# Gathered copies and ones-sums in the score ladder of a hybrid decoder layer

## The chip, the cores and the metric

The kernel runs on one core of a Trainium2 chip. The metric is device time in microseconds (us), the median of several runs; lower is better. One execution was profiled, and all durations below come from its trace.

## The reference

One decoder layer on x of 2048 tokens by 1024 channels, in float32: RMS norm, a wide projection, two groups of heads side by side, an output projection, then a gated MLP with a causal convolution and a final norm. The part that the change touches is the HGRN2 group, four heads with keys and values of 128:

```python
f = lb + (1.0 - lb) * jax.nn.sigmoid(hf)
k_hg = 1.0 - f
# S_t = diag(f_t) S_{t-1} + k_t v_t^T,  o_t = S_t^T q_t
o_hg = hgrn2_chunkwise(q_hg, k_hg, v_hg, log_f)
o_hg = rmsnorm(o_hg, hg_norm_w[l])
o_hg = o_hg * jax.nn.silu(hg)
```

Within a block of tokens the output of token t is a sum over earlier tokens s of a score times v_s, and the score is the sum over the 128 key channels of q_t * k_s times the product of all f between s and t. The second group is sliding-window attention with sinks (eight heads of 64, window 128).

## The kernel before

The 2048 tokens are worked off in two halves of 1024 (`hf`). Each half has a mix stage (attention and HGRN2 heads), then the output projection, gate and up, and down. All large matmuls split a float32 operand into a high and a low part of the type fp32r (a float32 form that the TensorE multiplies in one pass) and add three products; names ending in hi/lo, whi/wlo, XH/XL are such parts. A matmul of plain float32 shows two records in the trace.

In the mix stage `hgrn` and `attend` are generators, one of each per head `h` (0 to 3), advanced in turn. A planner inside the framework then sets the order of the instructions on each engine from its own cost estimates; the engines wait for each other through semaphores, and each engine works strictly in its order. So the order has to be read from the built program.

One head of `hgrn`: projections `f` and `hq` give f and q with the 128 key channels on partitions and 1024 tokens along the row; K = 1 - f and Q = q * f. The scores ST, eight blocks of 128 by 128 tokens, are filled in pieces:

- The diagonal (s = t): float32 matmuls of K with q per block into `pdiag` (L544), of which only the diagonal is kept (L545, a product with the identity).
- A ladder of levels m = 1, 2, 4 ... 64 (`LEVELS`). At level m tokens stand in pairs of neighbouring groups of m: the later group takes its scores from Q, the earlier from K. Matmuls write them to `plev`; then Q of the later groups and K of the earlier ones are multiplied by the running products of f (L609, L610), f is folded to half its length (L616), and the next level follows. So level 2m needs the products of level m.
- For m below 32, heads 0 to 2 work in pairs (`pairs`, `place_pairs`): ScalarE copies the needed half of K of two blocks into `KK` (L566), and four 128x128 matmuls serve eight blocks (L569). Half of the result lies m partitions too low; ScalarE copies it to `moved` (L576), a DMA on ScalarE's queue shifts it into `odd` (L579, and L581 for level 1), and VectorE places it with a mask (L588), the other half directly (L585). The last head doesn't pair: eight matmuls with 64 columns per level (L602), placed by L625.
- m = 32 and 64: small matmuls per block (L607), copied by ScalarE (L630).

Afterwards Kn is K transposed (`pkn`, L640), pu = Kn v (L647), the states SS follow, and per block two products go into `po` (L665, L666), each followed by its square with a sum over the row (L667). Their norm, a transposition (`pot`) and the gate give the head's output.

Beside it on TensorE stand the projections (`f`, `hq`, `q`, `g`, L212), `project_v` for two heads at once (`pvv`, L698 to L700, with 24 matmuls of 256 columns per block of tokens, evicted by ScalarE, L702), the attention (`psc` scores, `ppt` transpositions, `poT` outputs) and, at the stage's end, the output projection (`pop`). All score groups use the two PSUM banks of the pool "hg".

Of the kernel before, what the change touches and what calls it, by code (L numbers as in the profile page):

```python
# [43 lines left out]
KB = 2  # L44
# [6 lines left out]
def hymba_layer(ctx: ExitStack, tc: tile.TileContext, a: dict, out: bass.AP):  # L51
# [18 lines left out]
    def ps(kind, name):  # L70
        return spaces[kind].tile([P, 512], F32, tag=kind, name=name)
# [12 lines left out]
    nc.gpsimd.memset(eps, EPS)  # L84
    ident = cp.tile([P, P], F32, name="ident")
# [434 lines left out]
    def hgrn(hf, h, X, invb, vs, WG, mix, p, fu=None):  # L520
# [12 lines left out]
        K = p.tile([P, HALF], F32, tag="K", name="K", bufs=1)  # L533
        nc.vector.tensor_scalar(K, f, -1.0, 1.0, op0=ALU.mult, op1=ALU.add)
        Q = p.tile([P, HALF], F32, tag="Q", name="Q", bufs=1)
# [4 lines left out]
        for b in range(NB):  # L540
            pd = ps("hg", "pdiag")
            for i in range(4):
                c = slice((b * 4 + i) * P, (b * 4 + i + 1) * P)
                nc.tensor.matmul(pd[:, i * P:(i + 1) * P], K[:, c], q[:, c], start=True, stop=True)  # L544
            nc.vector.tensor_tensor(ST[:, 4 * b:4 * b + 4], pd.rearrange("p (i t) -> p i t", i=4),  # L545
                                    ident.unsqueeze(1).to_broadcast([P, 4, P]), op=ALU.mult)

# [12 lines left out]
        F, left = f, None  # L560

        def pairs():


            KK = p.tile([P, HALF // 2], F32, tag="KK", name="KK", bufs=KB)
            nc.scalar.copy(KK.rearrange("p (r b c m) -> p r c b m", r=TT // 2, c=2, m=m),  # L566
                           K.rearrange("p (r c b w m) -> p r c b w m", c=2, b=nbc, w=2, m=m)[:, :, :, :, 0])
            for r in range(TT // 2):
                marks[m] = nc.tensor.matmul(pl[:, r * P:(r + 1) * P], KK[:, r * P:(r + 1) * P],  # L569
                                            Qv[:, 2 * r * nbc:2 * (r + 1) * nbc, 1], start=True, stop=True)  # L570

        def place_pairs():

            plv = pl.rearrange("p (r c t) -> p r c t", r=TT // 2, c=2)
            moved, odd = [p.tile([P, TT // 2, 64], F32, tag="lv", name=n, bufs=LV) for n in ("moved", "odd")]
            nc.scalar.copy(moved, plv[:, :, 1])  # L576

            rows_ = P - max(m, 2)
            nc.scalar.dma_start(odd[0:rows_], moved[m:m + rows_])  # L579
            if m == 1:  # L580
                nc.scalar.dma_start(odd[rows_:rows_ + 1], moved[P - 1:P])  # L581
            STv = ST.rearrange("p (r c) (b w m) -> p r c b w m", c=2, w=2, m=m)
            mk = C.lmask[m].bitcast(U32).rearrange("p (b m) -> p b m", m=m)
            mk = mk.unsqueeze(1).to_broadcast([P, TT // 2, nbc, m])
            nc.vector.copy_predicated(STv[:, :, 0, :, 1], mk, plv[:, :, 0].rearrange("p r (b m) -> p r b m", m=m))  # L585
            r = slice(0, P - m)
            ov = odd[r].rearrange("p r (b m) -> p r b m", m=m)
            return lambda: nc.vector.copy_predicated(STv[r, :, 1, :, 1], mk[r], ov)  # L588

        for m in LEVELS:  # L590
            nb = HALF // (2 * m)
            nbc = 64 // m
            Qv = Q.rearrange("p (b w m) -> p b w m", w=2, m=m)
            Kv = K.rearrange("p (b w m) -> p b w m", w=2, m=m)
            Fv = F.rearrange("p (b w) -> p b w", w=2)
            pl = ps("hg", "plev")
            paired = m < 32 and h < HG - 1
            if paired:
                pairs()
            elif m < 32:  # L600
                for c in range(TT):
                    marks[m] = nc.tensor.matmul(pl[:, c * 64:(c + 1) * 64], K[:, c * P:(c + 1) * P],  # L602
                                                Qv[:, c * nbc:(c + 1) * nbc, 1], start=True, stop=True)
            else:
                for c in range(TT):
                    for s0 in range(0, P, 2 * m):
                        nc.tensor.matmul(pl[s0:s0 + m, c * m:(c + 1) * m], K[:, c * P + s0:c * P + s0 + m],  # L607
                                         Q[:, c * P + s0 + m:c * P + s0 + 2 * m], start=True, stop=True)
            nc.vector.tensor_tensor(Qv[:, :, 1], Qv[:, :, 1], Fv[:, :, 0:1].to_broadcast([P, nb, m]), op=ALU.mult)  # L609
            done = nc.vector.tensor_tensor(Kv[:, :, 0], Kv[:, :, 0], Fv[:, :, 1:2].to_broadcast([P, nb, m]), op=ALU.mult)  # L610
# [10 lines left out]
            if paired:  # L621
                left = place_pairs()
            elif m < 32:
                mk = C.lmask[m].bitcast(U32).rearrange("p (b m) -> p b m", m=m)
                nc.vector.copy_predicated(ST.rearrange("p c (b w m) -> p c b w m", w=2, m=m)[:, :, :, 1],  # L625
                                          mk.unsqueeze(1).to_broadcast([P, TT, nbc, m]),
                                          pl.rearrange("p (c b m) -> p c b m", c=TT, m=m))
            else:
                for s0 in range(0, P, 2 * m):
                    nc.scalar.copy(ST[s0:s0 + m, :, s0 + m:s0 + 2 * m],  # L630
                                   pl[s0:s0 + m, 0:TT * m].rearrange("p (c m) -> p c m", c=TT))
        yield
# [28 lines left out]
        for c in range(TT):  # L661
# [5 lines left out]
            nc.scalar.activation(on[:, c], o, AF.Square, accum_out=ss[:, c:c + 1])  # L667
# [626 lines left out]
```

## Time and profile before

| | |
|---|---|
| median of 3 runs | 2198.23 us (2197.66 to 2200.65) |
| profiled execution, first to last instruction | 2198.0 us |
| mean granted TensorE clock | 0.997 |
| TensorE (PE) busy | 2180.4 us, 99% |
| VectorE (DVE) busy | 1639.5 us, 75% |
| ScalarE (ACT) busy | 1049.9 us, 48% |
| mix stage of half 0 around the change | 68.2 to 402.0 us |
| mix stage of half 1 around the change | 1158.2 to 1495.0 us |

How rows are read: "L609 DVE TENSOR_TENSOR Q<-Q,f ..." is the code line, the engine, the operation, and what is written from what, with buffer numbers left out; then come the shapes (partitions x elements), the count, busy time and the mean of one in ns, and the idle time before with what ended it. In the timeline the first number is the start, the second the length, both in us. Waits are "engine line <- releaser: total, times, longest". POOL (GpSimd) is busy 6.3 us in all and plays no part. The profiled span lies 0.2 us under the median.

### The profile page before, as it was taken

What the parts mean: (1) busy time and instruction counts of PE and PEld (TensorE: products, weight loads), DVE (VectorE), ACT (ScalarE), POOL (GpSimd) and SP (SyncE); (2) the same over time, 40 slices, a digit from 0 to 9 for tenths busy, and PEclk for the clock granted to TensorE, in tenths of its full rate; (3) what the DMA queues carried; (4) which work ended last, traced back from release to release, by engine and by line L of the source; (5) the groups of instructions that cost most, each with busy time, mean ns of one, the idle gap of its engine ahead of it and who ended that gap; (6) DMA issues with size and microseconds to landing.
All of it is one profiled execution on the core that took longest, in us unless ns stands there. A gap on an engine that the chain in (4) does not pass through costs nothing.

```text
span 2198.0 us, 29524 instructions
## 1 busy us (share of the span) xinstructions
PE 2180.4 (99%) x11424; PEld 1834.0 (83%) x11424; DVE 1639.5 (75%) x2451; ACT 1049.9 (48%) x1848; POOL 6.3 (0%) x28
## 2 busy tenths in 40 slices
PE   9999999999999999999999999999999999999998
PEld 7988988888888888888889889888888888888888
DVE  6567568688887888885855666677888878887766
ACT  6445544454444445335735455544644444443353
POOL 1000000000000000000000000000000000000000
PEclk9999999999999999999999999999999999999999
DMA  4101112323333234964631111114132323259643
GB/s 155 51 32 48 39 41 68 119 74 102 104 109 108 89 127 143 372 241 156 209 125 41 44 36 51 58 39 134 58 125 92 125 91 109 98 183 393 233 144 130
DMA packets 94358, 257.91 MB, mean 117 GB/s; under 512 B 11594, under 2 KB 17546, under 8 KB 94218
## 3 DMA queue, kind: packets, MB, share of 16 engines
q1 hardware_dynamic: 88992, 251.30, 33.9%
q10 hardware_dynamic: 5226, 4.73, 0.7%
q8 instruction: 89, 1.46, 0.3%
q14 instruction: 51, 0.42, 0.1%
HBM read 195.10 MB, written 57.15 MB: 115 GB/s over the span
## 4 chain that ended last, share of the span: by engine, by line
PE 95%; DVE 3%; ACT 1%; DMA 1%; issue 0%; SPq 0%; DVEq 0%; ACTq 0%
PE X L877 7%; PE X L878 7%; PE X L879 7%; PE pop L212 7%; PE hq L212 4%; PE q L212 4%; PE f L212 4%; PE g L212 4%; PE Y L879 4%; PE Y L878 4%; PE Y L877 4%; PE pdx L1088 3%; PE pdx L1089 3%; PE pdx L1090 3%; PE pdy L1089 3%; PE pdy L1088 3%
## 5 line engine op out<-in xcount | busy, mean ns | idle before, releaser
L706 ACT CAST whi<-raw 128x1024 fp32r<-128x1024 f32 x88 | 92.6, 1053 | 109.2 <-PE X L878 68.2
L877 PE MATMUL X<-T,whi 128*128 128x512 f32 x352 | 136.9, 389 | 0.0
L878 PE MATMUL X<-T,whi 128*128 128x512 f32 x352 | 136.9, 389 | 0.0
L879 PE MATMUL X<-T,wlo 128*128 128x512 f32 x352 | 136.9, 389 | 0.0
L972 DVE SCALAR_TENSOR_TENSOR y<-ga,cw,y 128x1024 f32<-128x1024 f32 x88 | 112.5, 1281 | 26.0 <-ACT y L970 26.0
L884 ACT COPY u<-X 128x512 f32<-128x512 f32 x88 | 51.4, 585 | 133.3 <-PE X L879 133.1
L707 DVE TENSOR_TENSOR wlo<-raw,whi 128x1024 fp32r<-128x1024 f32 x88 | 107.3, 1220 | 0.0
L190 ACT CAST whi<-raw 128x1024 fp32r<-128x1024 f32 x57 | 59.5, 1048 | 93.1 <-PE q L212 31.9
L707 DVE TENSOR_TENSOR xld<-raw,xhd 128x1024 fp32r<-128x1024 f32 x72 | 80.8, 1133 | 19.1 <-ACT xhd L706 18.9
L706 ACT CAST xhd<-raw 128x1024 fp32r<-128x1024 f32 x72 | 69.7, 978 | 43.6 <-DMA raw<-act0T 14.8
L212 PE MATMUL pop<-XL,whi 128*128 128x512 f32 x256 | 86.1, 396 | 2.1 <-DVE XL L224 2.1
L212 PE MATMUL pop<-XH,wlo 128*128 128x512 f32 x256 | 85.2, 393 | 0.8 <-DVE wlo L191 0.8
L212 PE MATMUL pop<-XH,whi 128*128 128x512 f32 x256 | 84.5, 397 | 0.2
L878 PEld LDWEIGHTS X<-T,whi 128*128 128x128 f32 x352 | 66.1, 188 | 13.7
L877 PEld LDWEIGHTS X<-T,whi 128*128 128x128 f32 x352 | 66.1, 188 | 13.7
L879 PEld LDWEIGHTS X<-T,wlo 128*128 128x128 f32 x352 | 66.1, 188 | 13.7
L1088 PE MATMUL pdx<-xhd,hid 128*128 128x512 f32 x192 | 74.4, 391 | 1.0 <-ACT hid L706 1.0
L1089 PE MATMUL pdx<-xld,hid 128*128 128x512 f32 x192 | 74.7, 389 | 0.0
L1090 PE MATMUL pdx<-xhd,lod 128*128 128x512 f32 x192 | 73.7, 389 | 0.0
L698 PE MATMUL pvv<-whi,XH 128*128 128x256 f32 x256 | 73.5, 288 | 0.0
L191 DVE TENSOR_TENSOR wlo<-raw,whi 128x1024 fp32r<-128x1024 f32 x57 | 69.5, 1222 | 4.2 <-ACT whi L190 4.1
L699 PE MATMUL pvv<-whi,XL 128*128 128x256 f32 x256 | 72.6, 284 | 0.0
(379 smaller groups left out, 6563.3 us busy)
## 6 DMA issues: line engine op xcount, KB each, us to landing
wr<-in_w_down SPq DMA_DIRECT2D x90, 512.0 KB, 4.8
raw<-in_w_gate SPq DMA_DIRECT2D x44, 512.0 KB, 3.6
raw<-in_w_up SPq DMA_DIRECT2D x44, 512.0 KB, 3.6
raw<-act0T SPq DMA_DIRECT2D x20, 512.0 KB, 6.1
raw<-act1T SPq DMA_DIRECT2D x20, 512.0 KB, 10.1
act0B<-y SPq DMA_DIRECT2D x33, 256.0 KB, 2.6
act1B<-y SPq DMA_DIRECT2D x33, 256.0 KB, 2.4
raw<-in_w_out SPq DMA_DIRECT2D x16, 512.0 KB, 4.7
```

The costliest lines, as they stand in the source:

```text
L212: marks["unit"] = nc.tensor.matmul(o[b], w, x[:, bs], start=f, stop=l)
L698: nc.tensor.matmul(o[:, 0:256], xh[:, t], hi[:, c], start=kt == 0, stop=False)
L699: nc.tensor.matmul(o[:, 0:256], xl[:, t], hi[:, c], start=False, stop=False)
L706: return (nc.scalar.copy(h, src), (eng or nc.vector).tensor_tensor(l, src, h.bitcast(F32), op=ALU.subtract))
L707: (eng or nc.vector).tensor_tensor(l, src, h.bitcast(F32), op=ALU.subtract))
L877: nc.tensor.matmul(o, wh[:, ws], xh, start=i == 0 and not more, stop=False, skip_group_check=more)
L878: nc.tensor.matmul(o, wh[:, ws], xl, start=False, stop=False, skip_group_check=more)
L879: r = nc.tensor.matmul(o, wl[:, ws], xh, start=False, stop=i == 3, skip_group_check=more)
L972: nc.vector.scalar_tensor_tensor(y, g[:, w:w + HALF], C.cw[:, ft, w:w + 1], y, op0=ALU.mult, op1=ALU.add)
L1088: nc.tensor.matmul(o, wh[:, i, c], ah[:, i, cols], start=f, stop=False, skip_group_check=more)
L1089: nc.tensor.matmul(o, wh[:, i, c], al[:, i, cols], start=False, stop=False, skip_group_check=more)
L1090: nc.tensor.matmul(o, wl[:, i, c], ah[:, i, cols], start=False, stop=l, skip_group_check=more)
```

## The change

It does five things in `hgrn`:

1. Q and K become two halves of one tile QK, and per level one VectorE instruction (`own`) multiplies both in place of two.
2. At every level from 2 on ScalarE copies the needed parts of both Q and K into a gathered tile G (two buffers), and the matmuls read G alone, in all four heads with pairing: four 128x128 matmuls at levels 2 to 16 and also at 64, sixteen small ones at 32. A pair now joins block c with block c + 4 instead of two neighbours.
3. The diagonal and level 1, in which each token has one partner, become element products on VectorE (`dd`), split into fp32r high and low parts (cast on ScalarE, difference on VectorE), and summed over the channels by two fp32r matmuls of 512 columns with a matrix of ones: two such groups for the diagonal, one for level 1. Level 1 needs no shift and no DMA.
4. The eight squares of `po` stand in a loop of their own behind all products.
5. The tiles' room comes from a smaller dynamic DMA scratch (256 bytes).

```diff
-KB = 2
+GB = 2
...
+    ones_r = cp.tile([P, P], F32R, name="ones_r")
+    nc.vector.memset(ones_r.bitcast(F32), 1.0)
...
-        K = p.tile([P, HALF], F32, tag="K", name="K", bufs=1)
+        QK = p.tile([P, 2, HALF], F32, tag="QK", name="QK", bufs=1)
+        Q, K = QK[:, 0], QK[:, 1]
...
-        for b in range(NB):
-            pd = ps("hg", "pdiag")
-            for i in range(4):
-                c = slice((b * 4 + i) * P, (b * 4 + i + 1) * P)
-                nc.tensor.matmul(pd[:, i * P:(i + 1) * P], K[:, c], q[:, c], start=True, stop=True)
+        def summed_products(x, y):
+            d = p.tile([P, 512], F32, tag="dd", name="dd", bufs=2)
+            hi, lo = [p.tile([P, 512], F32R, tag="dg", name=n, bufs=4) for n in ("dh", "dl")]
+            nc.vector.tensor_tensor(d, x, y, op=ALU.mult)
+            nc.scalar.copy(hi, d)
+            nc.vector.tensor_tensor(lo, d, hi.bitcast(F32), op=ALU.subtract)
+            o = ps("hg", "pdiag")
+            nc.tensor.matmul(o, ones_r, hi, start=True, stop=False)
+            marks[1] = nc.tensor.matmul(o, ones_r, lo, start=False, stop=True)
+            return o
+        for b, bs in halves():
+            pd = summed_products(q[:, bs], K[:, bs])
...
+            if m > 1:
+                G = p.tile([P, 2, HALF // 2], F32, tag="G", name="G", bufs=GB)
+                nc.scalar.copy(G.rearrange("p t (b c m) -> p t b c m", c=2, m=m), far)
...
+                    for r in range(R):
+                        x = slice(r * P, (r + 1) * P)
+                        marks[m] = nc.tensor.matmul(pl[:, x], G[:, 1, x], G[:, 0, x], start=True, stop=True)
             else:
+                pl = summed_products(Q.rearrange("p (b w) -> p b w", w=2)[:, :, 1], K.rearrange("p (b w) -> p b w", w=2)[:, :, 0])
-            nc.vector.tensor_tensor(Qv[:, :, 1], Qv[:, :, 1], Fv[:, :, 0:1].to_broadcast([P, nb, m]), op=ALU.mult)
-            done = nc.vector.tensor_tensor(Kv[:, :, 0], Kv[:, :, 0], Fv[:, :, 1:2].to_broadcast([P, nb, m]), op=ALU.mult)
+            done = nc.vector.tensor_tensor(own, own, Fv.rearrange("p b w -> p w b").unsqueeze(3).to_broadcast([P, 2, nb, m]),
+                                           op=ALU.mult)
...
-            nc.scalar.activation(on[:, c], o, AF.Square, accum_out=ss[:, c:c + 1])
+        for c in range(TT):
+            nc.scalar.activation(on[:, c], po[c // 4][:, c % 4 * P:(c % 4 + 1) * P], AF.Square,
+                                 accum_out=ss[:, c:c + 1])
...
-    nc = bacc.Bacc("TRN2", target_bir_lowering=False, num_devices=1)
+    nc = bacc.Bacc("TRN2", target_bir_lowering=False, num_devices=1, dynamic_dma_scratch_size=256)
```

`far` is the view of QK that holds the later groups of Q and the earlier groups of K, with block c beside block c + 4; `place` moves and places a level as `place_pairs` did.

The planner orders the mix stages anew; outside them TensorE's order is the same row for row. Three places of the built order follow; tile names carry their buffer numbers where rows would read alike.

TensorE, first head of the first half, from the end of the projection q to the first pvv. Before:

```order
L212 MATMUL q1_544<-XL_276,whi_539 128x512
L212 MATMUL q0_543<-XH_275,wlo_540 128x512
L212 MATMUL q1_544<-XH_275,wlo_540 128x512
L544 MATMUL pdiag_615<-hg0_533,K_610 128x128 x4
L544 MATMUL pdiag_621<-hg0_533,K_610 128x128 x4
L698 MATMUL pvv_746<-whi_600,XH_146 128x256
```

Now, at the same place:

```order
L214 MATMUL q1_546<-XL_278,whi_541 128x512
L214 MATMUL q0_545<-XH_277,wlo_542 128x512
L214 MATMUL q1_546<-XH_277,wlo_542 128x512
L550 MATMUL pdiag_622<-dh_617,ones_r_87 128x512
L551 MATMUL pdiag_622<-dl_618,ones_r_87 128x512
L550 MATMUL pdiag_632<-dh_627,ones_r_87 128x512
L551 MATMUL pdiag_632<-dl_628,ones_r_87 128x512
L706 MATMUL pvv_745<-whi_602,XH_148 128x256
L707 MATMUL pvv_745<-whi_602,XL_149 128x256
```

Eight float32 matmuls have become four of fp32r in the same place; they now wait for VectorE's products and ScalarE's casts.

TensorE, last head of the first half, in the ladder (levels 4 and 8 before; levels 32 and 64 now), among attention and output projection. Before:

```order
L212 MATMUL pop1_3627<-XH_3134,wlo_3546 128x512
L602 MATMUL plev_3164<-Q_3037,K_3035 128x64 x8
L495 MATMUL ppt_3395<-ident_87,sc_3239 128x128 x4
L495 MATMUL ppt_3404<-ident_87,sc_3239 128x128 x4
L602 MATMUL plev_3177<-Q_3037,K_3035 128x64 x8
L506 MATMUL poT_3411<-po_3393,V_443 64x128
```

And now:

```order
L214 MATMUL pop1_3633<-XL_3123,whi_3551 128x512
L214 MATMUL pop0_3632<-XH_3122,wlo_3552 128x512
L604 MATMUL plev_3211<-G_3209 32x32 x16
L461 MATMUL psc_3314<-KS_444,qh_3308 128x256
L461 MATMUL psc_3314<-KS_444,ql_3309 128x256
L609 MATMUL plev_3235<-G_3233 128x128 x4
```

Before, a level of this head is eight matmuls and the ladder reaches to the transpositions of the attention (ppt); now a level is four, and the ladder ends while the attention still makes its scores (psc).

VectorE, third head, in the ladder from the product of level 8 on (the product is L609 and L610 before, L612 now; the last number of its shape is m). Before:

```order
L609 TENSOR_TENSOR Q<-Q,f 128x64x8
L477 TENSOR_SCALAR m<-m 128x8
L585 COPY_PREDICATED ST<-lmask_324,plev 128x4x8x8
L616 TENSOR_TENSOR f<-f 128x64
L610 TENSOR_TENSOR K<-K,f 128x32x16
L588 COPY_PREDICATED ST<-lmask_324,odd 120x4x8x8
L552 TENSOR_TENSOR hg_2081<-g_2670,invb 128x512
L552 TENSOR_TENSOR hg_2081<-g_2671,invb 128x512
L484 TENSOR_TENSOR den<-den,es 128x8
L485 RECIPROCAL den<-den 128x8
L468 COPY_PREDICATED sc<-own,psc 128x256
```

And now:

```order
L612 TENSOR_TENSOR QK<-QK,f 128x2x64x8
L586 COPY_PREDICATED ST<-lmask_318,odd 126x128x2
L619 TENSOR_TENSOR f<-f 128x64
L583 COPY_PREDICATED ST<-lmask_322,plev 128x64x4
L612 TENSOR_TENSOR QK<-QK,f 128x2x32x16
L586 COPY_PREDICATED ST<-lmask_322,odd 124x64x4
L583 COPY_PREDICATED ST<-lmask_326,plev 128x32x8
L619 TENSOR_TENSOR f<-f 128x32
L612 TENSOR_TENSOR QK<-QK,f 128x2x16x32
L586 COPY_PREDICATED ST<-lmask_326,odd 120x32x8
L583 COPY_PREDICATED ST<-lmask_330,plev 128x16x16
```

The levels follow each other closely now, and placements of shifted rows (L586, the tile odd) stand between two products where gate and attention work stood before.

73 lines of the change are left out of this document (32 added, 41 removed).

## The prediction

> **What bounds the kernel now.** I read the page's totals first, then its chain, then the two stages that the change touches, then what TensorE waits for in them.
>
> ```profile
> PE 2180.4 (99%) x11424; PEld 1834.0 (83%) x11424; DVE 1639.5 (75%) x2451; ACT 1049.9 (48%) x1848; POOL 6.3 (0%) x28
> ...
> PE 95%; DVE 3%; ACT 1%; DMA 1%; issue 0%; SPq 0%; DVEq 0%; ACTq 0%
> ```
>
> TensorE is busy 2180.4 of 2198.0 us and carries 95% of the chain that ends last. The changed code runs only in the two mix stages. The built orders of before and after agree row for row on TensorE outside them, so I cut the span there (columns: length, then PE, PEld, DVE, ACT, POOL busy, granted clock, DMA share, GB/s):
>
> ```profile
> 68.20:402.00 333.80, 331.64 (x2289) 289.05 (x2289) 224.35 (x440) 166.81 (x429) 0.00 (x0) 0.99 0.15 45
> ...
> 1158.20:1495.00 336.80, 334.72 (x2316) 291.59 (x2315) 225.68 (x439) 167.30 (x430) 0.00 (x0) 0.99 0.16 47
> ```
>
> TensorE is full there too (331.64 of 333.80, 334.72 of 336.80), VectorE at 67% and ScalarE at 50%. All that it waited for in these stages over 0.3 us, first stage, then second (total, times, longest):
>
> ```profile
> PE pop L212 <- DVE XL L224: 0.7, 1, 0.7
> PE plev L602 <- DVE K L610: 0.7, 1, 0.7
> ...
> PE pop L212 <- DVE XL L224: 1.4, 1, 1.4
> ```
>
> So the stage's length is the sum of its matmuls. A matmul taken away there is time taken away, as long as nobody feeds TensorE later than now.
>
> **What TensorE is spared.** I price a group by start to start: from its first matmul to the next other one, plus what that next one is late against its usual pitch. One plain fp32r 128x512 costs 10.88/48 = 0.227 us:
>
> ```profile
> 57.54 10.88 PE q L212 x48
> ```
>
> Score diagonal before (a float32 matmul leaves two records, so 8 make x16):
>
> ```profile
> 68.26 1.95 PE L544 MATMUL pdiag<-hg,K 128*128 128x128 f32 x16
> ...
> 69.96 0.36 PE L698 MATMUL pvv<-whi,XH 128*128 128x256 f32 x1
> ...
> 70.16 0.28 PE L699 MATMUL pvv<-whi,XL 128*128 128x256 f32 x1
> ```
>
> 69.96 - 68.26 = 1.70, and the next start follows after 0.20 where 0.12 is usual: 1.78 us. A pair-wise level, and the usual pitch of pvv (0.12):
>
> ```profile
> 73.52 0.28 PE L698 MATMUL pvv<-whi,XH 128*128 128x256 f32 x1
> 73.64 1.07 PE L569 MATMUL plev<-Q,KK 128*128 128x128 f32 x8
> 74.46 0.36 PE L699 MATMUL pvv<-whi,XL 128*128 128x256 f32 x1
> 74.66 0.28 PE L700 MATMUL pvv<-wlo,XH 128*128 128x256 f32 x1
> ```
>
> 0.82 + 0.08 = 0.90 us. A level of the last head, which isn't paired before:
>
> ```profile
> 346.72 1.90 PE L602 MATMUL plev<-Q,K 128*128 128x64 f32 x16
> 348.43 0.73 PE L212 MATMUL pop<-XL,whi 128*128 128x512 f32 x2
> 349.00 0.61 PE L212 MATMUL pop<-XH,wlo 128*128 128x512 f32 x2
> ```
>
> 1.71, and the two pop take 0.57 where 0.45 is usual: I take 1.79 (0.08 as above). Level 64:
>
> ```profile
> 99.01 1.15 PE L607 MATMUL plev<-Q,K 128*64 128x64 f32 x16
> 100.08 0.38 PE L459 MATMUL psc<-KS,ql 128*128 128x256 f32 x1
> 100.31 0.28 PE L459 MATMUL psc<-KS,qh 128*128 128x256 f32 x1
> ```
>
> 1.07 + 0.11 = 1.18 us. Now per head and half, 8 in all, 6 of them paired before:
> - diagonal: 1.78 becomes four fp32r 128x512, 0.91: 8 x 0.87 = 7.0
> - level 1: 0.90 (6 times) or 1.79 (twice) becomes two such matmuls, 0.45: 6 x 0.45 + 2 x 1.34 = 5.4
> - levels 2 to 16 of the last head: four groups of 1.79 become four of 0.90: 2 x 4 x 0.89 = 7.1
> - level 64: 1.18 becomes a group like a pair level, 0.90: 8 x 0.28 = 2.2
> - level 32 keeps 16 small matmuls, the other heads' levels 2 to 16 keep four 128x128: 0.
>
> Sum 21.7 us. The third term has a rule against it. By the Trainium skill, page "TensorE: Matmul & The Clock Gate", section "Back-to-back issue gap", a matmul's spacing grows with its streamed columns, so 64 columns would cost half of 128, halving the count would spare nothing, and the sum would be 14.6 (2183.4 us). The rows above deny it: 1.71/16 = 0.107 us per 64-column record, 0.82/8 = 0.103 per 128-column one. The same page's section on LDWEIGHTS (128 weight columns take 107 ns) fits them.
>
> **What the other engines get.** Prices:
>
> ```profile
> L536 DVE TENSOR_TENSOR Q<-hg,f 128x1024 f32<-128x1024 f32 x8 | 9.8, 1220 | 8.3 <-PE po L666 8.3
> L545 DVE TENSOR_TENSOR ST<-pdiag,ident 128x512 f32<-128x512 f32 x16 | 10.8, 688 | 11.5 <-PE pdiag L544 11.5
> L609 DVE TENSOR_TENSOR Q<-Q,f 128x512 f32<-128x512 f32 x56 | 38.6, 690 | 30.9 <-PE plev L569 18.6 <-PE plev L607 11.8 <-PE plev L602 0.4
> ...
> L585 DVE COPY_PREDICATED ST<-lmask,plev 128x256 f32<-128x256 uint32 x30 | 16.6, 554 | 3.4 <-ACT moved L576 3.3
> ```
> ```profile
> L706 ACT CAST whi<-raw 128x1024 fp32r<-128x1024 f32 x88 | 92.6, 1053 | 109.2 <-PE X L878 68.2 <-issue 19.1 <-PE Z L878 13.8
> ...
> L566 ACT COPY KK<-K 128x512 f32<-128x512 f32 x30 | 19.1, 636 | 29.6 <-DVE K L610 21.2 <-DVE K L534 8.2
> L667 ACT ACTIVATE on<-po 128x128 f32<-128x128 f32 x64 | 17.6, 275 | 58.3 <-PE po L666 56.9
> ...
> L576 ACT COPY moved<-plev 128x256 f32<-128x256 f32 x30 | 11.1, 371 | 23.8 <-PE plev L569 23.4
> ```
>
> VectorE, per head: fourteen products of 0.69 become seven of 1.22 (-1.1); three element products and three subtractions come (+4.1); placing stays within 1 us. That is +3 to +4, some 25 us over both stages: 475 of 649 us, 73%. ScalarE, per paired head: five copies of 0.64 become six gathers of 1.05 and three casts of 0.64 come, less one moved copy: +4.7; in the last head, which had none of it, +9.7; together 48 us, 382 of 649, 59%. Not in the trace is a gather or a level's product of 1024: between 1.05 (a plain cast of that size) and twice KK, 1.27; between 1.22 (Q from q and f, plain) and twice 0.69, 1.38. I take the lower ends, since KK and Q with their gaps already cost what plain ones of 512 do. Neither engine becomes the bound by its sum, so I cost both at nothing on the path; the cover is TensorE's own queue of projections, and if it runs out the price is the wait itself. ScalarE's queue issues six DMAs that shift rows per paired head now (two at level 1) and four then; the last head goes from none to four. SyncE's queue keeps its loads in nearly the same order and no load is added. ones_r is one memset ahead of the first load's landing: nothing. The smaller scratch moves no instruction.
>
> The ladder is where cover could end. A gather needs the previous level's product; with two G buffers the gather of level 8 also waits for level 2's matmuls. From there to level 64's matmuls a head needs four gathers, three products and seven handoffs, 8.6 us (4.2 + 3.7 + 0.7; 10.0 by the upper prices). A handoff I take as 0.1; K, which is done at 81.47 in the VectorE rows below, had its copy start at 81.50, and level 32 costs TensorE 0.63 + 0.10 = 0.73:
>
> ```profile
> 81.50 0.62 ACT L566 COPY KK<-K 128x512 f32<-128x512 f32 x1 [0.20 <-DVE K L610]
> ```
> ```profile
> 94.38 0.70 PE L607 MATMUL plev<-Q,K 128*32 128x32 f32 x32
> 95.01 0.38 PE L698 MATMUL pvv<-whi,XH 128*128 128x256 f32 x1
> 95.23 0.28 PE L699 MATMUL pvv<-whi,XL 128*128 128x256 f32 x1
> ```
>
>  TensorE's order puts between these two points, in the third head (the tightest), 70 pvv x 0.12 + three levels x 0.90 + level 32 0.7 = 11.8 us; by the same count some 14 in the first head and more in the other two. Spare in the third: 3.2 us, of which three moved copies (1.1), four evictions of v and the DMA issues on ScalarE eat most, partly beside VectorE's products. So it holds, by 1 or 2 us.
>
> What a shifted level costs the queue behind it: VectorE's placement of the shifted rows waits for a DMA, and the next product stands behind it.
>
> ```profile
> 78.89 0.73 DVE L609 TENSOR_TENSOR Q<-Q,f 128x512 f32<-128x512 f32 x1
> ...
> 80.78 0.69 DVE L610 TENSOR_TENSOR K<-K,f 128x512 f32<-128x512 f32 x1
> 81.79 0.74 DVE L588 COPY_PREDICATED ST<-lmask,odd 126x256 f32<-126x256 uint32 x1 [0.33 <-DMA odd<-moved]
> ```
>
> The level's matmuls were done at 78.89, the rows had landed at 81.79: 2.9 us with the copy (0.37), so 2.5 for issue and landing. It stands within the 11.8.
>
> Squares behind the products: eight squares, 8 x 0.28 plus their accumulator reads, now start together after the last product instead of beside it; rsqrt and pot come some 3 us later. In the last head's order TensorE has ppt, poT and 23 pop between, of which the pop alone are 5.2 us: nothing.
>
> Against the profiled execution: 2198.0 - 21.7 = 2176.3. The median shown, 2198.23, is 0.2 above that span, so 2176.5. The unknowns around it: all old waits of these stages gone, -3.6; and the clock, which twice fell to half:
>
> ```profile
> 368.30:371.70 3.40, 3.40 (x28) 2.74 (x25) 2.58 (x6) 0.31 (x1) 0.00 (x0) 0.50 0.00 0
> 1440.10:1443.50 3.40, 3.40 (x9) 2.62 (x9) 3.40 (x7) 0.00 (x0) 0.00 (x0) 0.51 0.70 170
> ```
>
> Each such 3.4 us stretch (the Trainium skill, "TensorE: Matmul & The Clock Gate", Part 1, gives 3413 ns as the gate's window; the rows agree) does half the work and costs 1.7: both gone -3.4, four new ones +7. So 2169 to the one side; to the other 1 to 2 us of wait in each of eight heads, 8 to 15: 2191.
>
> **Rivals.**
> 1. The ladder outruns its cover. If every gather stands behind two evictions of v (0.6) and every product behind a placement (0.44), the third head's 8.6 becomes 12.4 against 11.8, and the first head comes near; with a late landing on top, 1 to 4 us in half of the heads: 2182 to 2193. For it: VectorE's and ScalarE's orders are denser there. Against: TensorE hardly waited before.
> 2. Slower: the shifted rows land late. In the ladder two of the products stand behind such a placement. If issue and landing took 6 instead of 2.5 us, a head would lose 7 less its spare: some 6 in the first and third, 1 in the others, 28 in all, 2204. It decides from just under 6 us on, where the loss passes 26. Against: DMA share 0.15 in these stages and the 2.5 measured.
> 3. The change doesn't do what it says: the 48 summing matmuls run as full float32. Their kind is in the trace:
>
> ```profile
> L284 PE MATMUL pinv<-invb,ones 128*128 128x512 f32 x18 | 8.5, 591 | 0.0
> ```
>
> A record lasts 591 against about 390 ns, so pitch 0.43, two records: 48 x (0.86 - 0.23) = 30 us, 2206. Against: the operands are typed fp32r like the projections'.
> 4. The page's column rule: 2183.4, denied by rows that price both forms; it gets 1%.
>
> **How the numbers follow.** A change of this kernel under 0.2%, 4.4 us, can't be told from none: "faster" is below 2193.8, "slower" above 2202.6. Forecast (2169 to 2182) 0.67; rival 1 up to 2193.8 0.18, beyond it, within 0.2%, 0.06; rival 2 0.05 and 3 0.03, both slower; rival 4 0.01, faster. Faster 0.86, same 0.06, slower 0.08. The range 2169 to 2191 leaves out about 0.18.
>
> **What would show it.** Right: four pdiag of 0.227 us pitch, last-head levels with 8 records, stages of about 323 and 326 us, waits of TensorE there still under 5 us. Wrong: TensorE waiting at plev for G (ladder), VectorE idle before the shifted placement for over 3 us (landing), pdiag records of 590 ns (float32), or more stretches at half clock.

## The result, and the profile after

The changed kernel takes 2173.75 us (2171.3 to 2174.83) against 2197.94 us (2197.41 to 2200.65) of the kernel before, run beside it: a ratio of 0.9887, 95% interval 0.9873 to 0.9901. The forecast was 2176.5, with 2169 to 2191 around it. The profiled execution spans 2173.1 us; it is the run of 2174.83, so a run's time lies 1.7 us above its span.

The totals and the chain that ended last, from the page of the changed kernel:

```profile
PE 2151.3 (99%) x11136; PEld 1809.6 (83%) x11136; DVE 1659.9 (76%) x2446; ACT 1094.1 (50%) x1902; POOL 6.0 (0%) x28
...
PE 93%; DVE 3%; ACT 2%; DMA 1%; issue 1%; SPq 0%; ACTq 0%; DVEq 0%
```

TensorE has 288 matmul records fewer and is busy 29.1 us less; VectorE and ScalarE took on 20.4 and 44.2 us. TensorE is still the bound.

The two mix stages, cut at the same instructions as before (length, PE, PEld, DVE, ACT, POOL busy, granted clock, DMA share, GB/s):

```profile
68.15:388.10 319.95, 316.27 (x2140) 276.03 (x2139) 228.18 (x430) 186.41 (x454) 0.00 (x0) 1.00 0.16 48
1145.45:1469.30 323.85, 320.27 (x2170) 279.46 (x2169) 230.55 (x428) 189.92 (x459) 0.00 (x0) 1.00 0.16 51
```

They were 333.80 and 336.80: 26.8 us less, while the span fell by 24.9. The remaining +1.9 us lies outside them. Score diagonal in the first head of the timeline, and the group rows of the new work:

```profile
68.18 0.40 PE L550 MATMUL pdiag<-dh,ones_r 128*128 128x512 f32 x1
68.42 0.40 PE L551 MATMUL pdiag<-dl,ones_r 128*128 128x512 f32 x1
68.65 0.39 PE L550 MATMUL pdiag<-dh,ones_r 128*128 128x512 f32 x1
68.88 0.40 PE L551 MATMUL pdiag<-dl,ones_r 128*128 128x512 f32 x1
69.11 0.28 PE L706 MATMUL pvv<-whi,XH 128*128 128x256 f32 x1
```
```profile
L612 DVE TENSOR_TENSOR QK<-QK,f 128x1024 f32<-128x1024 f32 x56 | 68.5, 1223 | 8.2 <-ACT G L598 7.6
L598 ACT COPY G<-QK 128x1024 f32<-128x1024 f32 x48 | 51.5, 1073 | 28.5 <-DVE QK L612 26.5 <-DVE ST L583 1.8
L586 DVE COPY_PREDICATED ST<-lmask,odd 126x256 f32<-126x256 uint32 (+3 forms) x32 | 16.6, 519 | 9.2 <-DMA odd<-moved 9.1
```

Four summing matmuls start 0.23 apart; the diagonal takes 0.93 us where it took 1.78. A level's product takes 1.22, a gather 1.07. The shifted rows keep VectorE waiting for 9.1 us in the whole run, at most 1.2 at a time.

What TensorE waits for in the stages over 0.3 us in total, first stage, then second (total, times, longest):

```profile
PE poT L508 <- DVE pp L500: 1.7, 2, 1.5
PE pu L653 <- ACT Kn L647: 1.4, 1, 1.4
PE poT L508 <- DVE po L500: 0.5, 2, 0.4
...
PE poT L508 <- DVE pp L500: 1.8, 3, 1.5
PE pu L653 <- ACT Kn L647: 1.1, 1, 1.1
PE poT L508 <- DVE po L500: 0.5, 2, 0.4
```

None of them is a matmul waiting for a gather. All 7.0 us stand in the last head, where the attention's softmax and Kn are late. And in this execution TensorE's clock did not fall after them, as it had twice before:

```profile
363.40:366.80 3.40, 2.99 (x34) 2.42 (x35) 3.08 (x10) 1.93 (x10) 0.00 (x0) 1.00 0.00 0
1441.30:1444.70 3.40, 2.88 (x35) 2.23 (x36) 3.02 (x9) 1.99 (x11) 0.00 (x0) 1.00 0.00 0
```

### The profile page after: what moved, and what is told of

Read it like the earlier page. It is cut to its first block, busy times and chain, and to the rows that moved or that the text cites. A ratio compares the mean times of both kernels' runs of the same rounds, so it can differ in the third digit from the quotient of the medians.

```text
span 2173.1 us, 29038 instructions
## 1 busy us (share of the span) xinstructions
PE 2151.3 (99%) x11136; PEld 1809.6 (83%) x11136; DVE 1659.9 (76%) x2446; ACT 1094.1 (50%) x1902; POOL 6.0 (0%) x28
## 4 chain that ended last, share of the span: by engine, by line
PE 93%; DVE 3%; ACT 2%; DMA 1%; issue 1%; SPq 0%; ACTq 0%; DVEq 0%
PE X L885 7%; PE pop L214 7%; PE X L887 7%; PE X L886 7%; PE hq L214 4%; PE f L214 4%; PE q L214 4%; PE g L214 4%; PE Y L885 4%; PE Y L886 4%; PE Y L887 4%; PE pdx L1098 3%; PE pdx L1096 3%; PE pdx L1097 3%; PE pdy L1096 3%; PE pdy L1097 3%
## 5 line engine op out<-in xcount | busy, mean ns | idle before, releaser
L715 DVE TENSOR_TENSOR xld<-raw,xhd 128x1024 fp32r<-128x1024 f32 x72 | 80.9, 1132 | 21.7 <-ACT xhd L714 21.2
L612 DVE TENSOR_TENSOR QK<-QK,f 128x1024 f32<-128x1024 f32 x56 | 68.5, 1223 | 8.2 <-ACT G L598 7.6
```

What stands on the lines that cost most here:

```text
L715: (eng or nc.vector).tensor_tensor(l, src, h.bitcast(F32), op=ALU.subtract))
```

## The experiments

Theory A after the result was the prediction's: the time fell by the matmuls taken away, and the squares' place was worth nothing. The rivals were that the squares' place, the ladder's cover or the clock had made the difference. The kernel before took 2198.24 us beside the first four runs, 2198.16 beside the next four and 2199.32 beside the last three, and each ratio is to that. Differences to the changed kernel are between medians, to its 2173.75. For the whole gain the clock falls out as a rival: the mean granted clock of the runs beside the experiments was 0.997 to 1.000 in the kernel before and that of the changed kernel's runs 0.998 and 0.999; a thousandth is 2.2 us.

**The last head without pairs.** Levels 2 to 16 of the last head as eight matmuls of 64 columns again.

```diff
+                alone = m < 32 and h == HG - 1
...
+                if alone:
+                    for c in range(TT):
+                        marks[m] = nc.tensor.matmul(pl[:, c * 64:(c + 1) * 64], K[:, c * P:(c + 1) * P],
+                                                    Qv[:, c * nbc:(c + 1) * nbc, 1], start=True, stop=True)
```

> The changed kernel with one part undone: the last head's levels 2 to 16 are again eight float32 matmuls of 64 columns each from Q and K themselves, placed whole from PSUM. Theory (the time is the sum of TensorE's groups): 2 halves x 4 levels x (1.79 - 0.90) = 7.1 us slower than the changed kernel, about 2180.9 us; its groups again 0.107 us per record, 16 records. The profiled gain was 3.2 us more than the 21.7 of the sum, and the two stretches at half clock in the last heads (3.4 us) are gone. If the long ladder of the last head is what lowers the clock there, one or two such stretches come back and the loss is 8.8 to 10.5 us (up to 2184). Rival (price by streamed columns): no difference to the changed kernel, 2173.7 us.

Measured: 2184.53 us (2182.83 to 2190.15), ratio 0.9942 (0.9929 to 0.9956), 10.8 more than the changed kernel. So halving the count of a level's matmuls does spare their time, though the columns double: the column rule of the prediction's fourth rival falls by a run. It is 3.7 more than the matmuls' 7.1; TensorE waits 9.7 us in these stages instead of 7.0, 1.3 of it in each stage at a matmul of the ladder for its gather, the sign that the prediction gave for rival 1. No half-clock stretch came back there.

**The diagonal as matmuls again, in all heads.**

```diff
-            pd = summed_products(q[:, bs], K[:, bs])
+            pd = ps("hg", "pdiag")
+            for i in range(4):
+                c = slice((b * 4 + i) * P, (b * 4 + i + 1) * P)
+                nc.tensor.matmul(pd[:, i * P:(i + 1) * P], K[:, c], q[:, c], start=True, stop=True)
```

> The changed kernel with the score diagonal again as eight float32 128x128 matmuls of K with q per head, no products, casts and differences for it; level 1 stays a sum by ones. Theory: 8 x (1.78 - 0.91) = 7.0 us slower than the changed kernel, about 2180.7 us, although VectorE is spared 16 x 1.37 us and ScalarE 16 x 0.62 us. Rival (VectorE's and ScalarE's added work is on the path in part): under 4 us slower, or faster.

Measured: 2176.84 us (2176.15 to 2176.92), ratio 0.9901 (0.9888 to 0.9915): 3.1 more, not 7.0. The matmuls did come back (pdiag takes 6.1 us more, start to start), but the waits in the stages fell from 7.0 to 3.6 us, those of the last heads from 7.0 to 2.2. Part of what the sums by ones spare is paid back there as a wait for the engines that form the products. How large a part is not settled: by the medians the rival holds, yet in the two profiles the stages together are 5.4 us longer with the matmuls. The spans differ by only 1.8 us because the changed kernel's execution spent 3.2 us more between the stages, where both kernels have the same rows (the last section comes back to this).

**The squares beside their products again**, the one line of the loop moved back:

```diff
+            nc.scalar.activation(on[:, c], o, AF.Square, accum_out=ss[:, c:c + 1])
-        for c in range(TT):
-            nc.scalar.activation(on[:, c], po[c // 4][:, c % 4 * P:(c % 4 + 1) * P], AF.Square,
-                                 accum_out=ss[:, c:c + 1])
```

> The changed kernel with each square of po again right behind its product. Theory: cost and gain nothing on the path, 2173.7 us within 2 us. Rival (the squares kept the products apart, and TensorE's last wait for pot): 2 to 5 us slower than the changed kernel.

Measured: 2194.67 us (2190.74 to 2197.79), ratio 0.9983 (0.9974 to 0.9992). An edit that the prediction costed at nothing is worth 21 us; with everything else of the change in place, only 3.5 us of gain are left. The trace shows how. In the built order each product of a PSUM bank (L671 and L672 together make one) now waits for the square of the one before it in that bank; behind the products it waits for none (Activation_49 is the semaphore that ScalarE raises):

```
L671 MATMUL po<-v,ST 128x128 [waits Activation_49]
L672 MATMUL po<-SS,QK 128x128
L671 MATMUL po<-v,ST 128x128 [waits Activation_49]
L672 MATMUL po<-SS,QK 128x128
```

The planner fills the time between with projections and attention, so a head's products spread. Products of the first head, first and last start at the end of "to", first with squares beside, then in the changed kernel:

```profile
L671 PE MATMUL po<-v,ST x16: 270/275/275, 114.2 to 133.9; 128*128 128x128 f32 x16
```
```profile
L671 PE MATMUL po<-v,ST x16: 270/275/275, 114.2 to 117.9; 128*128 128x128 f32 x16
```

They hold both banks of the "hg" pool for some 20 us instead of 4, and the next head's scores need those banks. In the first stage the second head's first scores start 0.4 us later than in the changed kernel, the third's 13.6 and the last one's 28.1. That the held banks make the heads late is argued from this order and not shown by a run; the second head is hardly late, though the first head held the banks as long. The last head's first scores, diagonal and level 1, with squares beside and in the changed kernel:

```profile
L550 PE MATMUL pdiag<-dh,ones_r x3: 498/605/628, 346.9 to 350.8; 128*128 128x512 f32 x3
```
```profile
L550 PE MATMUL pdiag<-dh,ones_r x3: 392/404/404, 318.8 to 330.6; 128*128 128x512 f32 x3
```

What TensorE would have run beside the last ladder is then gone. It waits (both stages) and its clock falls for twice 6.8 us:

```profile
PE psc L461 <- DVE sc L470: 4.1, 4, 2.0
PE pdiag L550 <- ACT dh L547: 1.5, 1, 1.5
...
PE psc L461 <- DVE sc L470: 3.5, 4, 1.3
PE pop L214 <- ACT XH L225: 2.0, 1, 2.0
```
```profile
341.20:348.00 6.80, 5.50 (x23) 5.31 (x24) 6.49 (x16) 3.75 (x8) 0.00 (x0) 0.52 0.25 77
1423.70:1430.50 6.80, 5.11 (x22) 4.53 (x23) 6.74 (x16) 4.06 (x8) 0.00 (x0) 0.52 0.25 77
```

Taking from each matmul's distance to the next its usual one, the excess between 320 us and 420 us of the trace (second stage: the same stretch, counted from its first projection) is 32.1 us over both stages, against 13.4 in the changed kernel. These 18.7 are nearly all of the 19.7 by which the stages are longer. The loss lies in the last head as a whole, in many small waits and in the half clock, and not at one place. The profiled execution is the fastest of this kernel's eleven runs (2190.74 us). Their granted clock is on record too, and on the whole it is the lower, the longer the run: 0.996 at 2190.74, 0.994 at the median, 0.992 at 2197.79. A thousandth of such a run is 2.2 us, so at the median the clock takes some 13 us, against 2 to 4 in the changed kernel: as an estimate, about half of the 21 us is time at half clock.

The wait itself was a rule that could have been read. By the Trainium skill, page "PSUM — Partial Sum Buffer", section "PSUM bank collisions raise a hardware error", a PSUM bank must not be touched by two engines at the same time in the same partitions, even where their columns differ, so software puts a dependency between them. The waits in the built order agree; what a collision does isn't shown by any run here.

**Kn of the last head copied by VectorE**, to take one of the two long waits of the changed kernel's last heads away.

```diff
-            nc.scalar.copy(Kn[:, 4 * b:4 * b + 4].rearrange("p a b -> p (a b)"), pk)
+            (nc.vector.tensor_copy if h == HG - 1 else nc.scalar.copy)(
+                Kn[:, 4 * b:4 * b + 4].rearrange("p a b -> p (a b)"), pk)
```

> The changed kernel, with the last head's copy of Kn from PSUM on VectorE, which idles 4.8 us there, instead of ScalarE, where it stands behind eight exponentials. In the changed kernel TensorE waits for that copy 2.5 us in all and for the attention's masks 4.6 us right after. Theory: the 2.5 us go, 2171.2 us; if the masks come earlier as well, 2168. Rival: the planner orders the end of the stage anew and the wait moves to the masks, same time.

Measured: 2174.07 us (2173.04 to 2176.58), ratio 0.9891 (0.9878 to 0.9905): no difference, as the rival had it. The wait of pu went, and waits of 4.6 us came at the transpositions of the attention:

```profile
PE ppt L497 <- DVE sc L488: 2.6, 2, 2.3
...
PE ppt L497 <- DVE sc L488: 2.0, 1, 2.0
```

**The kernel before with the squares behind, alone.** The same three lines, in the kernel before.

> The kernel before with one edit: the eight squares of a head stand behind the eight products, as in the changed kernel; diagonal and levels stay as before. Theory A (TensorE's groups and the squares are two gains that need each other): TensorE waits for only 3.6 us in the stages of the kernel before and loses 3.4 us to half clock there, so moving the squares can bring no more than these 7 us: 2191 to 2197, though the products of a head draw together from some 17 us to some 4. Theory B (the squares alone carry the 21 us that the changed kernel loses when they go back beside the products): about 2177. Theory C (the square's place matters only where the groups are short): 2198, as before.

Measured: 2203.44 us (2200.35 to 2204.55), ratio 1.0021 (1.0012 to 1.0030): slower. Theory B is out, but A and C missed too. The profiled execution (2198.6) shows the banks coming free early, yet no gain from it; the last head's diagonal starts at 325.2 instead of 342.8, while its ladder ends only 3.5 us earlier (376.0 after 379.5). In the kernel before, and with the squares behind:

```profile
L544 PE MATMUL pdiag<-hg,K x16: 275/275/377, 342.8 to 345.2; 128*128 128x128 f32 x16
...
L607 PE MATMUL plev<-Q,K x48: 196/196/222, 376.2 to 379.5; 128*32 128x32 f32 x32, 128*64 128x64 f32 x16
```
```profile
L544 PE MATMUL pdiag<-hg,K x16: 270/275/275, 325.2 to 326.9; 128*128 128x128 f32 x16
...
L607 PE MATMUL plev<-Q,K x48: 196/196/315, 369.6 to 376.0; 128*32 128x32 f32 x32, 128*64 128x64 f32 x16
```

At its end TensorE waits, 4.6 and 5.1 us in the two stages, most of it for one high part of the output projection and a maximum of the attention:

```profile
PE pop L212 <- ACT XH L516: 1.8, 1, 1.8
PE poT L506 <- DVE m L474: 1.2, 1, 1.2
```

The profiled execution is the fastest of the eleven runs (2200.35 us, granted clock 0.998); the median lies 3.1 us above it, and the slowest, 2204.55, had a clock of 0.996. So, as an estimate, most of that distance is the clock again: 0.002 of the run is 4.4 us. The four corners together: before 2198.2; only the squares moved 2203.4; only the levels and the diagonal changed 2194.7; both 2173.75. The squares alone cost 5.2 us, the levels and the diagonal alone gain 3.5, and some 26 us of the gain of 24 come from the two together.

**The squares behind the four products of their bank.**

```diff
+            if c % 4 == 3:
+                for i in range(c - 3, c + 1):
+                    nc.scalar.activation(on[:, i], po[i // 4][:, i % 4 * P:(i % 4 + 1) * P], AF.Square,
+                                         accum_out=ss[:, i:i + 1])
```

> The changed kernel with the four squares of each PSUM bank right behind the four products of that bank, instead of all eight behind all eight. No product then waits for a square of its own bank. Theory A (what costs is the wait of a product for the square before it in the same bank, which spreads a head's products over 17 to 24 us and holds both banks that long): as the changed kernel, 2174, with the products of a head within 8 us. Rival B (what costs is any square ahead of a product in ScalarE's order, by the work that it pushes back): half of the 21 us, about 2184 or more.

Measured: 2174.08 us (2173.41 to 2175.91), ratio 0.9887 (0.9871 to 0.9903), the changed kernel's own. The products of the first head start at 114.2 to 117.9 (L671) again. So the eight need not stand together; it is enough that no product waits for a square of its bank. (The squares ran behind the last product here too, so this doesn't tell what a square between two banks' products would cost if ScalarE came to it earlier.)

**Each gather copied twice.**

```diff
+                for _ in range(2):
+                    nc.scalar.copy(G.rearrange("p t (b c m) -> p t b c m", c=2, m=m), far)
```

> The changed kernel with each gather of K and Q copied twice, so each level's matmuls and the next product wait one gather (1.05 to 1.27 us) more; ScalarE gets 56 x 1.07 = 60 us more and stands at about 61% of the stages plus some. Theory A (the ladder has little spare: 8.6 us needed, 11.8 us of cover in the third head): the third head needs 8.6 + 4 x 1.07 = 12.9 and lacks 1 us, others lack nothing, and later heads start later; 2175 to 2184. Rival B (the ladder has wide spare, since the planner starts it early): within 1 us of 2174. Rival C (ladder decides): each of eight heads loses 4 us, 2206.

Measured: 2184.00 us (2183.42 to 2186.85), ratio 0.9935 (0.9922 to 0.9948): 10.3 more. The size is at theory A's upper end, the place isn't where A had it. The third head, the one with the least cover by the prediction's count, lost little: the last head behind it starts 0.6 and 0.5 us later in its stage than in the changed kernel. What TensorE waits for over half a microsecond stands in the last head, most of it at the ladder's end (both stages):

```profile
PE pkn L647 <- ACT ST L637: 3.0, 1, 3.0
...
PE pkn L647 <- ACT ST L637: 3.2, 1, 3.2
PE poT L508 <- DVE pp L500: 2.5, 4, 1.1
```

L637 copies level 64's scores. In ScalarE's row it now stands behind a table load and eight exponentials of the softmax, which it led in the changed kernel; it starts as the last of them ends. In the changed kernel, then here:

```profile
352.82 0.37 ACT L636 COPY ST<-plev 64x256 f32<-64x256 f32 x1
353.21 1.28 ACT L485 ACT_TABLE_LOAD   x1
```
```profile
355.60 1.28 ACT L485 ACT_TABLE_LOAD   x1
...
359.71 0.39 ACT L483 ACTIVATE sc<-sc,m 128x128 f32<-128x128 f32 x1
360.00 0.19 ACT L483 ACTIVATION_READ_ACCUMULATOR sc<-sc,m 128x1 f32 x1
360.09 0.73 ACT L637 COPY ST<-plev 64x256 f32<-64x256 f32 x2
```

A chain made a little longer lost its place in another engine's order, which the planner sets, and paid the length of what stood there. The stages are 9.9 us longer in sum; the waits in them grew by 5.1, and the clock fell to half once in each last head (at 361.9 and 1443.9), 1.7 us each.

**The shifted rows by two DMAs.**

```diff
-            nc.scalar.dma_start(odd[0:P - m], moved[m:P])
+            way = dp.tile([P, R, 64], F32, name=f"way{hf}{h}{m}")
+            nc.scalar.dma_start(way[0:P - m], moved[m:P])
+            nc.scalar.dma_start(odd[0:P - m], way[0:P - m])
```

> The changed kernel with the rows of each shifted level moved by two DMAs, one behind the other, through another tile: issue and landing go from about 2.5 to about 5 us at four levels of each head, and the placement of the shifted rows, with the product behind it on VectorE, waits as much longer if it stands there early. Theory A (the landing is covered up to nearly 6 us): 2174 to 2178. Rival B (each landing stands in the ladder): two levels x 2.5 us x 8 heads less 3.2 us spare in each, up to 2188.

Measured: 2193.14 us (2192.29 to 2199.04), ratio 0.9983 (0.9974 to 0.9991): 19.4 more. Theory A falls, and B was too small. VectorE's placement waits for the rows, 35.8 us instead of 9.1 in all:

```profile
DVE ST L588 <- DMA odd<-way: 35.8, 24, 2.8
```

In the first head this stands in the ladder: the product of level 32, behind the rows of level 4, starts at 88.44 there and at 86.06 in the changed kernel. The experiment isn't pure, for the second DMA waits on ScalarE's queue for the first and holds it up (the copies `moved` wait 8.4 us for that in the first stage). That a landing is covered up to nearly 6 us, as theory A had it, isn't shown by this; with the way doubled most of the gain is gone.

**The diagonal as matmuls in the last head only.** What the second experiment suggests: keep the sums where they spare time, and take them away where they turn into a wait.

```diff
+            if h < HG - 1:
+                pd = summed_products(q[:, bs], K[:, bs])
+            else:
+                pd = ps("hg", "pdiag")
+                ...
```

> The changed kernel with the score diagonal as float32 matmuls in the last head of each stage alone; the three other heads keep the sums by ones. In the last heads TensorE of the changed kernel waits 7.0 us for ScalarE and VectorE; with the diagonal as matmuls in all heads those waits fell and TensorE's added 7.0 us cost only 3.1. Theory A (what was spared in the last head turned into a wait there): the last heads' two groups add 2 x 0.87 = 1.7 us and take 2 to 4 us of wait away, so 2171 to 2174, as fast as the changed kernel or up to 2.5 us faster. Rival B (the waits do not hang on the last head's diagonal): 2173.75 + 1.7 = 2175.5.

Measured: 2170.21 us (2169.11 to 2170.69), ratio 0.9865 (0.9852 to 0.9879): 3.5 under the changed kernel, whose runs begin at 2171.3, and below theory A's 2171 to 2174. The stages are 319.80 and 322.45 long, 1.55 us less in sum; the waits in them fell from 7.0 to 2.6:

```profile
PE pkn L652 <- ACT ST L638: 0.5, 1, 0.5
PE poT L508 <- DVE po L500: 0.4, 1, 0.4
PE psc L461 <- DVE sc L470: 0.4, 1, 0.4
...
PE poT L508 <- DVE po L500: 0.6, 2, 0.4
```

So 1.55 us of the gain, with the waits that went, is shown to be the edit's. The other 3 us of the two profiles lie between the stages, where the changed kernel's execution had short waits and a half-clock stretch that this one didn't have. The rows there are the same in both kernels, and such a stretch comes and goes there between executions (last section), so that part is hardly the edit's. The whole 3.5 us is also less than the 4.4 that the prediction took as the least that can be told from none.

**Diagonal and level 1 as matmuls**, level 1 in pairs on a gather and with a shift. The edits are those of the second experiment, the condition `m > 1` taken away from the gather, and the shift and placing of level 1 done as for the other levels, with one more DMA for its last row.

> The changed kernel with both element products undone: the diagonal as eight float32 matmuls of two records, level 1 as four pair-wise matmuls on gathered copies like levels 2 to 16, with its shift. Theory A (each term of the sum holds and lies on the path): diagonal 8 x 0.87 = 7.0, level 1 8 x 0.45 = 3.6, together 10.6: 2184.4. Theory B (the diagonal alone cost 3.1 when it went back, since waits in the last heads fell; level 1 in full): 2173.75 + 3.1 + 3.6 = 2180.5. Rival C (a fifth shifted level in the ladder and a gather more make each head's chain 3 to 4 us longer, and it shows): 2188 or more.

Measured: 2183.83 us (2182.08 to 2185.74), ratio 0.9927 (0.9915 to 0.9940): 10.1 more. Theory A's 10.6 fits, with a mixture behind it: start to start, pdiag and plev hold 9.3 us more, TensorE waits 2.3 and 2.1 us at pkn for the end of the last ladder, which has one gather and one shift more, and the clock fell to half once in the first stage. That the longer ladder is the reason for these waits is likely, not shown.

**One buffer for the gathers.**

```diff
-GB = 2
+GB = 1
```

> The changed kernel with one buffer for the gathered copies instead of two: each gather waits for the matmuls of the level before, not the one two before. Theory A (TensorE's time hangs on how early the last head's levels start, since behind them little other work is left; in the built order they come some 20 us later than in the changed kernel): waits and half-clock stretches in the last heads as with the squares beside the products, 2185 to 2195. Rival B (a gather waits 0.8 us per level more and nothing else): within 3 us of 2174.

Measured: 2185.83 us (2185.32 to 2189.46), ratio 0.9940 (0.9926 to 0.9953): 12.1 more, theory A. The products stay close together (within 6 us) here, and yet the ladders come later. Last head's first scores, first stage:

```profile
L550 PE MATMUL pdiag<-dh,ones_r x3: 393/393/404, 339.4 to 345.8; 128*128 128x512 f32 x3
```

Counted from the beginning of its stage, the last head starts 20.1 us later than in the changed kernel in the first stage, which is 11.4 us longer, and 1.0 us later in the second, which is 2.5 us longer. So in this order a late last head costs, also where no spread of products made it late. It doesn't hold the other way round: in the kernel before, the squares behind brought the last head 18 us forward and gained nothing.

## Why the prediction was right, point by point

**TensorE's sum was right.** 21.7 us were forecast; start to start over all rows of the stages, pdiag with level 1 fell from 14.4 to 11.3 us and plev from 55.7 to 37.4: 21.4. The rest of the stages fell by 5.4: pop by 6.0, which before held the 2.1 us of its two waits and a part of the half-clock stretches, while all other rows together rose by 0.6, the new waits among them. Hence 320 and 324 us instead of the 323 and 326 of the forecast, and 2173.75 instead of 2176.5: the prediction had listed these two unknowns with -3.6 and -3.4 and left them out of the middle value. The 0.2 us that it put between span and median isn't the distance of a run from its own span, which is 1.7; the profiled execution of before was some 1.5 us slower than the median. VectorE and ScalarE took on 8.7 and 42.2 us in the stages where 25 and 48 were priced, and neither came near the bound.

**The step that failed: "Squares behind the products", "nothing".** With everything else done it is worth 21 us, and in the kernel before alone it is worth nothing. The prediction counted eight squares and asked who waits for the norm; it didn't ask what a square holds back, which is the next product of its bank, nor for whom the bank is then missing, the next head's scores. A row of the profile before bore on it: ScalarE's squares (L667) were idle 56.9 us waiting for po, a trace of the spread of the products. In the changed kernel this is 6.0:

```profile
L674 ACT ACTIVATE on<-po 128x128 f32<-128x128 f32 x64 | 16.9, 290 | 6.0 <-PE po L672 6.0
```

**"A matmul taken away there is time taken away, as long as nobody feeds TensorE later than now"** holds, and its condition was the whole question. That the forecast came out is in part luck, for what kept the condition true was a term put at nothing. With the squares beside, 21.4 us of matmuls would have brought 3.5; TensorE runs dry in the last head. The waits of before (3.6 us) didn't show this, since the matmuls now removed were themselves the cover.

**The ladder (rival 1) and the landing (rival 2).** No matmul of the changed kernel waits for a gather, the third head held, and landing keeps VectorE for at most 1.2 us at a time. But their prices were mis-sized: a third head with 4.3 us more lost about half the microsecond that the count gave it, the last head, counted as roomy, lost about 5 a stage; and a longer landing decides earlier than "just under 6 us": with the way doubled, which also held ScalarE's queue, the gain was down to 5 us. Rival 2 was a nearer danger than its 0.05.

**The float32 rival (3)** is out: the summing records last 398 and 396 ns, not 590. **The column rule (4)** is out by the rows and by the unpaired last head. By the Trainium skill, page "TensorE: Matmul & The Clock Gate", section "Back-to-back issue gap", that rule holds for a matmul standing alone, and in a stream the weight load sets the spacing too. So the section isn't against the rows, 0.107 and 0.103 us per record; the prediction took only the one rule from it.

**The signs.** Four pdiag at 0.23, eight records per level in the last head and the stages' lengths came as forecast; "waits under 5 us" did not, they are 7.0, new ones in the last head, and the runs with the diagonal as matmuls show that the added products are a reason for most of them.

## What to carry to other kernels

Where the bound engine hardly waits, removing its work pays only as far as the rest is covered by what remains; find the place where it would run dry first (here the last head, where no next head follows) and price edits there by themselves. An instruction of another engine that reads an accumulator bank between two matmuls into it can cost far more than its own time: the matmuls are spread, and whoever needs the bank next may come late. Here that was 21 us in one order and nothing in another, so it has to be tried in the order at hand. And an edit that is good in the other rounds can turn into a wait in the last one, where a mixed form had the lowest time, by 3.5 us, of which 1.55 are shown to be its own.

## What the runs showed of the hardware that was not expected

The granted clock falls to half for 3.4 us after waits far shorter than that, and not always. The kernel with the squares per bank has the changed kernel's waits, 1.6 us and 1.5 us some 5 us apart in the first stage:

```profile
PE poT L508 <- DVE pp L500: 1.7, 2, 1.5
PE pu L653 <- ACT Kn L647: 1.6, 1, 1.6
...
364.40:367.80 3.40, 3.40 (x27) 3.07 (x28) 2.21 (x7) 2.80 (x15) 0.00 (x0) 0.52 0.00 0
1442.90:1446.30 3.40, 3.40 (x28) 3.07 (x25) 1.32 (x4) 3.33 (x17) 0.00 (x0) 0.50 0.00 0
```

It fell to half in both stages; the changed kernel, with 1.4 and 1.5, stayed at 1.00 in both. Each of these is one execution: two of the changed kernel's four runs show a mean clock of 0.998 where the profiled one had 0.999, so it may have fallen in those. No wait in the stages of any of these profiles reached 3.4 us. If one counts steps of 3.41 us from a stretch at half clock in the same trace, the waits ahead of the two falls add up to 1.8 and 2.0 us in one step, while in the changed kernel they lie across two steps, 1.3 at most in one. That may be the difference; no run tests it, and the kernel before fell after a single wait of 0.7.

The clock also fell where TensorE hardly waited. Between the stages, 24 matmuls of one column (pst) stand close together, 2.5 us of TensorE's time. In 5 of the 13 profiled executions the clock fell to half at their end, with no wait of over 0.2 us in the 10 us ahead; in the other eight, with the same rows, it stayed at 1.00. In the changed kernel, just behind them:

```profile
1097.40:1099.10 1.70, 1.70 (x5) 1.32 (x4) 1.67 (x4) 0.11 (x1) 0.00 (x0) 0.50 0.01 1
```

So what a wait of this size costs, itself or itself and 1.7 us, was not to be told ahead, and 1.7 us between two executions need not belong to an edit.
